# Streaming Conformer layer on one core: the fourth product of odd feed-forward gates placed ahead of the third, and output rows stored from ScalarE's queue

## The chip, the cores and the metric

The kernel runs on one core of a Trainium2 chip. The metric is device time in microseconds (us). The core's engines work in parallel, each through its own instructions in order: TensorE (PE; its weight loads are listed apart as PEld), VectorE (DVE), ScalarE (ACT), GpSimd (POOL) and SyncE (SP), which here does little but issue DMAs. They wait for each other on semaphores. Matrix products end in banks of PSUM; weights and activations lie in SBUF.

## The reference

One layer works on 2048 prompt tokens and 64 sample tokens, all in fp32:

```
h = rms_norm(x) * (1 + sc1) + sh1                  # sc, sh, gt come from c @ w_ada
glu_a, glu_b, q, k, v, g_conv, g_attn = split(h @ w_in)
conv_out = silu(layer_norm(dwconv31(glu_a * sigmoid(glu_b)))) @ w_conv_out
attn_out = band_attention(norm(q), norm(k), v) @ w_attn_out    # 64-token chunks, own and 8 before
merged = sigmoid(g_conv) * conv_out + sigmoid(g_attn) * attn_out
x  = x + gt1 * (merged @ w_o)
h2 = rms_norm(x) * (1 + sc2) + sh2
gate, up = split(h2 @ w_ffn_in)                    # 2 x 2816 columns
y  = x + gt2 * ((silu(gate) * up) @ w_ffn_out)
```

`D_MODEL` is 1024. The outputs are y for both token sets, and the new convolution, key and value states.

## The kernel before

**Products.** Every fp32 weight is split into a high part (`whi`, made by ScalarE) and the rest (`wlo`, made by GpSimd, or by VectorE where the planner finds GpSimd too far behind). A product of fp32 matrices is then three matmuls: high by high, low by high, high by low.

**Stages.** The first part, up to about 1300 us, does the modulation, the input projection, convolution and attention for all tokens. Then three blocks of columns (tokens 0 to 576, 576 to 1344, 1344 to 2112, called blocks 0, 1 and 2) go one after the other through the merge (weights `ca`, matmuls `ps<-cin`), the output projection (`w_o`, matmuls `pw<-whi,m`), the residual and norm, and the feed-forward. The last half tiles of a block's feed-forward, the stores of its output and the loads of the next block's merge weights meet at the border of two blocks.

**The feed-forward.** Its 2816 columns are 22 gates f of 128. Gate and up projection of one f are done together with seven products instead of eight: sums of weight halves (`s1` to `s4`) and plain halves (`a11`, `a12`, `a22`) are multiplied with sums and plain halves of the activations (`t1` to `t4`, `b11`, `b21`, `b22`), each for half of the block's columns (288 in block 0, 384 in the others), twelve matmuls a product. `up` (line 1926) issues them. From f = 5 on (`EARLY`), s2, s1 and s4 of a gate add to one bank, `y`, which the a11 product of the gate before has begun; s3 and a22 add to a second one, `z`; a12 has a third, `x`. ScalarE copies `y` to `u2` after s2 and `z` to `v` after s3; s1 adds to `y` and so waits for the copy `u2`. VectorE adds `y` to `v` after s1, makes c1 from `x` after a12, and multiplies gate and up. The hidden rows are then multiplied with `w_ffn_out`: in block 0 by `down` after each pair of gates (matmuls `pd<-whi,hid`, added to `acc` by VectorE), in blocks 1 and 2 by `down_pair`, whose pieces lie between the products of the next pair at the places of `dn_at`; `down` ends each block.

**Order.** `up_operands` gives the order of the seven products, `weight_order` the order in which weight slabs are staged (two operands of `up_operands` to a slab, low and high, five slabs held), and `up` must follow it. Loads go out on SyncE's queue. Every DMA of SyncE and ScalarE takes one of eight hardware semaphores in turn (`DMAHW0` to `DMAHW7`), and waits for the DMA eight places before it. The planner (`stream`) places prefetches and stores in program order by its own estimate of time; the stores of the output rows (line 2021) are placed by `stream.at` some time after VectorE's last addition.

Of the kernel before, what the change touches and what calls it, by code (L numbers as in the profile page):

```python
# [28 lines left out]
NF = FFN // P  # L29
# [30 lines left out]
EARLY = 5  # L60
PAIRS = range(4, NF - 2, 2)
# [17 lines left out]
def tile_chunks(lo, hi):  # L79

    tiles = token_tiles(lo, hi)
    t, n = tiles[(len(tiles) + 1) // 2 - 1]
    return [(lo, t + n), (t + n, hi)]
# [24 lines left out]
class Lane:  # L108
# [17 lines left out]
    def step(self, entry):  # L126
        try:
            got = next(entry[0])
        except StopIteration:
            self.gens.remove(entry)  # L130
            return
        entry[1], entry[2] = got if isinstance(got, tuple) else (got, {})
# [407 lines left out]
def up_operands(f):  # L540

    ops = (["s2", "s3", "s1"] if f else ["s3", "s2", "s1"]) + ["a12"] * (f >= EARLY) + ["a22"] + ["a11"] * (EARLY <= f + 1 < NF) + ["s4"]
    return [(f + (op == "a11"), op) for op in ops]


def dn_at(f):

    return (0, 1, 3, 6 if f == PAIRS[-1] else 4)  # L550


def mod_order():
# [34 lines left out]
def streaming_layer(ctx: ExitStack, tc: tile.TileContext, I, O):  # L588
    nc = tc.nc
# [8 lines left out]
    y_p, y_s, cs_p, ks_p, vs_p, cs_s, kn_s, vn_s = O  # L598
    y_p, y_s, cs_p, cs_s = y_p[0], y_s[0], cs_p[0, 0], cs_s[0, 0]
# [4 lines left out]
    def rows(prompt, sample, t, n):  # L604
        return prompt[t - SMP : t - SMP + n] if t >= SMP else sample[t : t + n]
# [459 lines left out]
    def half_piece(i, name):  # L1065
        return (wc, wk)[i].tile([P, CW // 2], F32, tag=f"tg{i}", name=name, bufs=2 + i)
# [532 lines left out]
    def piece(tag, name):  # L1599
        return wk.tile([P, CW // 2], F32, tag=tag, name=name, bufs={"t1": 2, "t2": 3}[tag])  # L1600
# [117 lines left out]
    c0, c1 = tile_chunks(*CBLOCKS[0])  # L1718
# [3 lines left out]
    for s, (lo, hi) in enumerate(CBLOCKS):  # L1722
# [60 lines left out]
        def product(ps, w, b, first, last):  # L1783

            for k in range(4):
                mm3(
                    ps[:, :half], w[0][:, k], w[1][:, k], hs[b][0][:, k, :half], hs[b][1][:, k, :half],
                    first and k == 0, last and k == 3, skip_group_check=True,
                )

        def bank(tag):
            return ps_g.tile([P, 512], F32, tag=tag, name="ps", bufs=4)[:, :half]

        def copy(dst, src):
            stream.after("act", "pe")
            act.activation(dst, src, AF.Copy)

        def plus(dst, ps, b):
            stream.after("dve", "pe", "act")
            dve.tensor_tensor(dst, ps, b, ALU.add)  # L1800

        def silu(dst, z):

            tg = half_piece(0, "tg")[:, :half]
            stream.after("act", "pe", "dve")
            act.activation(tg, z, AF.Tanh, scale=0.5)
            stream.after("dve", "act")
            dve.scalar_tensor_tensor(dst, tg, 1.0, z, ALU.add, ALU.mult)
# [25 lines left out]
        def plain(f, i, ps):  # L1834
            hidden(f, i, ps)
            yield 1
# [83 lines left out]
        def rest_of_late(n=99):  # L1920
            while late and n:
                n -= 1
                if next(late[0], None) is None:
                    late.pop(0)

        def up(f, ops, at):
            def step(ps, op, b, first, last, e=f):
                product(ps, ops.use(e, op), b, first, last)
                ops.done()

            if f < EARLY:
                s1, c1 = (t[:, :half] for t in early[f])
                y = bank("y")
            else:
                y, s1 = begun.pop(f)
                c1 = s1

            z = None
            if not f:
                z = bank("y")  # L1940
                step(z, "s3", "t3", True, False)
            step(y, "s2", "t2", f < EARLY, False)
            rest_of_late(1)
            u2 = piece("t1", "u2")[:, :half]
            keep = (lambda dst, ps: plus(dst, ps, s1)) if f < EARLY else copy
            keep(u2, y)
            if f % 2:
                at(3)
            if f:
                z = bank("y")  # L1950
                step(z, "s3", "t3", True, False)
            v = half_piece(1, "v")[:, :half]
            keep(v, z)
            rest_of_late()
            if f % 2 == 0:
                at(0)
            step(y, "s1", "t1", False, False)
            plus(v, y, v)
            if f % 2:
                at(4)  # L1960
            if f >= EARLY:
                x = bank("gp")
                step(x, "a12", "b21", True, True)
                plus(x, x, s1)
                silu(c1, x)
            if f % 2 == 0:
                at(1)
            step(z, "a22", "t4", False, True)
            plus(z, z, u2)
            two = s and f - f % 2 in PAIRS  # L1970
            dve.tensor_tensor(z, z, c1, ALU.mult)
            if EARLY <= f + 1 < NF:
                ny = bank("y")
                step(ny, "a11", "b11", True, False, f + 1)
                begun[f + 1] = ny, piece("t2", "s1")[:, :half]
                copy(begun[f + 1][1], ny)
            for _ in paired(f, 0, z, c1) if two else [hidden(f, 0, z)]:
                pass
            step(y, "s4", "b22", False, True)
            if f < EARLY:  # L1980
                plus(y, y, s1)
            silu(y, y)
            dve.tensor_tensor(y, y, v, ALU.mult)
            late.append(paired(f, 1, y, v) if two else plain(f, 1, y))

        def down(fs, ws):

            last = fs[-1] == NF - 1
            for i, (t, n) in enumerate(tiles):
                if fs[0] == 0:  # L1990
                    acc[i] = token_row("acc")
                pss = [ps_g.tile([P, 512], F32, tag="gp", name="pd", bufs=4) for _ in range(2)]
                gt = gt2[int(t < SMP)] if last else None
                final = last and hi == T and i == len(tiles) - 1
                x1 = [x1s[q // 3][:n, q % 3] for q in (2 * i, 2 * i + 1)] if last else None
                if final:
                    for j in range(2):
                        dst = acc[i][:n, 512 * j : 512 * j + 512]
                        dve.tensor_tensor(dst, dst, gt[:n, 512 * j : 512 * j + 512], ALU.mult)
                        dve.tensor_tensor(dst, dst, x1[j], ALU.add)  # L2000
                for e, j in [(e, j) for e in fs for j in range(2)] if last and not i else [(e, j) for j in range(2) for e in fs]:
                    h = rows_of(e, t, n)
                    f = slice(512 * j, 512 * j + 512)
                    w = ws[e - fs[0]]
                    mm3(pss[j][:n], *h, w[0][:, 0, f], w[1][:, 0, f], e == fs[0], e == fs[-1])
                for j, ps in enumerate(pss):
                    f = slice(512 * j, 512 * j + 512)
                    dst = acc[i][:n, f]
                    stream.after("dve", "pe")
                    if fs[0] == 0:  # L2010
                        act.activation(dst, ps[:n], AF.Copy)
                    elif not last:
                        dve.tensor_tensor(dst, dst, ps[:n], ALU.add)
                    else:
                        if not final:
                            dve.tensor_tensor(ps[:n], ps[:n], dst, ALU.add)
                        dve.tensor_tensor(ps[:n], ps[:n], gt[:n, f], ALU.mult)
                        dve.tensor_tensor(dst, ps[:n], dst if final else x1[j], ALU.add)
                        stream.at(
                            stream.when("dve") + OUT_LAG,  # L2020
                            lambda t=t, n=n, f=f, dst=dst: nc.sync.dma_start(rows(y_p, y_s, t, n)[:, f], dst),
                        )
            for _ in fs:
                W.done()
# [30 lines left out]
        for f in range(0, NF, 2):  # L2055
            ops = Operands(f)
# [5 lines left out]
            def at(i, f=f):  # L2062
                if s and f - 2 in PAIRS:
                    if i in dn_at(f - 2):
                        down_pair(f - 2, dn_at(f - 2).index(i))
                elif i == 0 and 2 <= f <= NF - 4:
                    down([f - 2, f - 1], [W.get(("fo", e)) for e in (f - 2, f - 1)])
# [48 lines left out]
```

## Time and profile before

| | us |
|---|---|
| median of 3 runs | 3044.03 (3043.26 to 3046.47) |
| the profiled execution's own time | 3045.71 |
| its span | 3043.9 |
| TensorE busy | 2932.8 |
| VectorE busy | 1996.2 |
| ScalarE busy | 1321.8 |
| GpSimd busy | 984.2 |

Busy time overlaps between engines. A row of the timeline gives the start in us, the duration, engine, line, operation, output<-inputs by the program's names, shapes and a count where rows of one kind are folded; in brackets stand the idle time of the engine before it and what ended it. Nearly all rows have line L103, that of the helper which records each instruction, so the names tell them apart: `ps<-t` is a product with t1 to t4, `ps<-b` one with b11, b21 or b22, `pd<-whi,hid` is the down-projection, `u<-ps` and `v<-ps` are ScalarE's copies, `out<-acc` are the output stores, `tg<-g_d` loads of the merge's gates. A q behind an engine's name (SPq) means its queue of issued DMAs.

### The profile page before, as it was taken

Reading aid. Unit: us, or ns where it says so; the run is one execution under the profiler, and the core shown is the slowest. Engines: PE = TensorE matmul, PEld = TensorE weight load, DVE = VectorE, ACT = ScalarE, POOL = GpSimd, SP = SyncE. Lnnn points to the kernel's source line nnn. Section 1 sums busy time; section 2 is a strip of 40 time slices with the busy share of each in tenths; the row PEclk is TensorE's granted clock in tenths of the full one; section 3 lists DMA queues with packets and bytes.
Section 4 is the critical chain, followed back from the end, with each engine's and each line's share of the span. In section 5 each row is a group of like instructions: output and inputs, shape, how many; then the busy total and the mean of one; then the engine's idle time right before and its main releaser. Section 6 shows DMA issues by size and latency. Waiting matters only on the chain. (4 is left out here: it accounts for less than half of the span.)

```text
span 3043.9 us, 44749 instructions
## 1 busy us (share of the span) xinstructions
PE 2932.8 (96%) x16259; PEld 2609.7 (86%) x16259; DVE 1996.2 (66%) x3595; ACT 1321.8 (43%) x2371; POOL 984.2 (32%) x617
## 2 busy tenths in 40 slices
PE   7989898999999999989999999999999999999998
PEld 4889776887888888878989889999999898999997
DVE  5896687667956895566666755655666756366567
ACT  3334542563365257463444425534444244333332
POOL 1200120101011102345677433247767341333331
PEclk9999998999999999999999999999999999999999
DMA  9788798877997788886444786455556965355544
GB/s 304 261 278 285 254 298 296 273 246 264 299 289 222 267 270 267 257 278 216 148 144 143 233 283 206 159 164 190 184 194 202 340 213 191 118 167 174 166 161 176
DMA packets 487018, 690.97 MB, mean 227 GB/s; under 512 B 38420, under 2 KB 316808, under 8 KB 486797
## 3 DMA queue, kind: packets, MB, share of 16 engines
q1 hardware_dynamic: 474517, 670.72, 67.2%
q10 hardware_dynamic: 12280, 17.39, 1.6%
q8 instruction: 128, 2.10, 0.3%
q14 instruction: 93, 0.76, 0.1%
HBM read 503.79 MB, written 184.19 MB: 226 GB/s over the span
## 5 line engine op out<-in xcount | busy, mean ns | idle before, releaser
L103 POOL TENSOR_TENSOR wlo<-wst,whi 128x1024 fp32r<-128x1024 f32 (+1 forms) x180 | 401.7, 2238 | 497.6 <-ACT whi L103 452.2
L103 PE MATMUL ps<-t,whi 128*128 128x384 f32 (+1 forms) x2112 | 507.4, 325 | 10.9 <-DVE t L103 5.2
L103 PE MATMUL pd<-whi,hid 128*128 128x512 f32 (+1 forms) x1400 | 450.6, 392 | 3.3 <-DVE acc L103 3.3
L103 ACT ACTIVATE whi<-wst 128x1024 fp32r<-128x1024 f32 (+1 forms) x273 | 266.1, 979 | 356.7 <-PE ps L103 123.4
L103 PE MATMUL ps<-b,whi 128*128 128x384 f32 (+1 forms) x1584 | 381.1, 326 | 11.6 <-DVE pw L103 4.0
L103 PEld LDWEIGHTS ps<-t,whi 128*128 128x128 f32 x2112 | 371.8, 190 | 19.2 <-DVE t L103 6.2
L103 DVE SCALAR_TENSOR_TENSOR y<-u,wd,y 128x512 f32<-128x512 f32 (+1 forms) x480 | 369.2, 773 | 8.2
L103 PE MATMUL ps<-hh,whi 128*128 128x512 f32 (+2 forms) x992 | 364.5, 367 | 1.0 <-DMA whi<-w_din_h 0.8
L103 PE MATMUL ps<-hl,whi 128*128 128x512 f32 (+2 forms) x992 | 346.9, 350 | 0.0
L103 PE MATMUL ps<-hh,wlo 128*128 128x512 f32 (+2 forms) x992 | 346.9, 350 | 0.0
L103 DVE TENSOR_TENSOR acc<-acc,pd 128x512 f32<-128x512 f32 (+1 forms) x440 | 290.7, 684 | 80.5 <-PE pd L103 76.7
L103 PE MATMUL ps<-t,wlo 128*128 128x384 f32 (+1 forms) x1056 | 341.6, 324 | 0.0
L103 PEld LDWEIGHTS pd<-whi,hid 128*128 128x128 f32 (+1 forms) x1400 | 258.4, 185 | 64.4 <-DVE acc L103 6.8
L103 PEld LDWEIGHTS ps<-b,whi 128*128 128x128 f32 x1584 | 277.9, 189 | 14.9 <-DVE pw L103 4.3
L103 PE MATMUL pd<-wlo,hid 128*128 128x512 f32 (+1 forms) x700 | 274.1, 392 | 0.0
L103 PE MATMUL ps<-b,wlo 128*128 128x384 f32 (+1 forms) x792 | 257.4, 325 | 0.0
L103 ACT ACTIVATE pr<-pr,sm 128x640 f32<-128x640 f32 (+3 forms) x272 | 200.1, 747 | 128.1 <-DVE sm L103 126.2
L103 POOL TENSOR_TENSOR r<-t,mhalf 128x1 f32<-128x1 f32 (+3 forms) x68 | 82.2, 1211 | 412.8 <-DVE t L103 369.1
L103 PEld LDWEIGHTS ps<-hh,wlo 128*128 128x128 f32 x992 | 188.2, 190 | 22.5 <-issue 0.4
L103 POOL TENSOR_TENSOR wlo<-wup,whi 128x1024 fp32r<-128x1024 f32 (+1 forms) x64 | 138.2, 2161 | 212.5 <-ACT whi L103 196.7
L103 PEld LDWEIGHTS ps<-hh,whi 128*128 128x128 f32 x992 | 189.1, 191 | 20.0 <-issue 2.7
L103 PEld LDWEIGHTS ps<-hl,whi 128*128 128x128 f32 x992 | 189.1, 191 | 15.5 <-issue 1.7
(215 smaller groups left out, 5719.6 us busy)
## 6 DMA issues: line engine op xcount, KB each, us to landing
whi<-w_din_h SPq DMA_DIRECT2D x72, 512.0 KB, 4.1
wlo<-w_din_l SPq DMA_DIRECT2D x72, 512.0 KB, 7.1
wst<-sum_d SPq DMA_DIRECT2D x131, 256.0 KB, 2.9
wmod<-in_w_ada SPq DMA_DIRECT2D x48, 512.0 KB, 7.2
sum_d<-ws SPq DMA_DIRECT2D x88, 256.0 KB, 2.5
wst<-in_w_ffn_in SPq DMA_DIRECT2D x85, 256.0 KB, 3.5
wst<-in_w_in SPq DMA_DIRECT2D x40, 512.0 KB, 7.4
wst<-in_w_ffn_in SPq DMA_DIRECT2D x37, 512.0 KB, 5.5
```

Source lines behind the costliest of these rows:

```text
L103: return f(*args, **kw)
```

## The change

In odd gates from f = 5 on, the product a12 with what VectorE and ScalarE make of it moves ahead of s1, and the operands' order with it, so that the slabs of such a gate are (s3, a12) and (s1, a22) instead of (s3, s1) and (a12, a22). The last piece of `down_pair`, B22, stays behind s1, at the fifth slab's place instead of the fourth's. Even gates keep their order. The 34 output stores are issued by ScalarE instead of SyncE.

```diff
@@ up_operands, dn_at
-    ops = (["s2", "s3", "s1"] if f else ["s3", "s2", "s1"]) + ["a12"] * (f >= EARLY) + ["a22"] + ["a11"] * (EARLY <= f + 1 < NF) + ["s4"]
+    ops = (["s2", "s3"] if f else ["s3", "s2"]) + ["a12"] * (f >= EARLY and f % 2) + ["s1"] + ["a12"] * (f >= EARLY and f % 2 == 0) + ["a22"] + ["a11"] * (EARLY <= f + 1 < NF) + ["s4"]
     return [(f + (op == "a11"), op) for op in ops]
...
-    return (0, 1, 3, 6 if f == PAIRS[-1] else 4)
+    return (0, 1, 3, 6 if f == PAIRS[-1] else 5)
@@ up
+            def factor():
+                if f >= EARLY:
+                    x = bank("gp")
+                    step(x, "a12", "b21", True, True)
+                    plus(x, x, s1)
+                    silu(c1, x)
+
             if f % 2 == 0:
                 at(0)
+            else:
+                factor()
             step(y, "s1", "t1", False, False)
             plus(v, y, v)
             if f % 2:
-                at(4)
-            if f >= EARLY:
-                x = bank("gp")
-                step(x, "a12", "b21", True, True)
-                plus(x, x, s1)
-                silu(c1, x)
-            if f % 2 == 0:
+                at(5)
+            else:
+                factor()
                 at(1)
             step(z, "a22", "t4", False, True)
@@ down
-                            lambda t=t, n=n, f=f, dst=dst: nc.sync.dma_start(rows(y_p, y_s, t, n)[:, f], dst),
+                            lambda t=t, n=n, f=f, dst=dst: nc.scalar.dma_start(rows(y_p, y_s, t, n)[:, f], dst),
```

First place: TensorE in an odd gate of block 0. Of each product the first matmul is shown, or the first that waits; t3, t1, b21 and t4 belong to s3, s1, a12 and a22, b11 to a11 of the next gate. First before, then the change.

```order
L103 MATMUL ps_16850<-t3_13835,wlo_16727 128x288 [waits Pool_49]
...
L103 MATMUL ps_16784<-t1_13829,whi_16726 128x288 [waits Activation_49]
...
L103 MATMUL ps_16883<-b21_12991,wlo_16733 128x288 [waits Pool_49]
...
L103 MATMUL ps_16850<-t4_13837,whi_16732 128x288 [waits Activation_49]
...
L103 MATMUL ps_16920<-b11_12989,whi_16770 128x288 [waits DVE_49]
```

```order
L103 MATMUL ps_16850<-t3_13835,wlo_16727 128x288 [waits Pool_49]
...
L103 MATMUL ps_16869<-b21_12991,wlo_16727 128x288
...
L103 MATMUL ps_16784<-t1_13829,whi_16732 128x288 [waits Activation_49]
...
L103 MATMUL ps_16850<-t4_13837,whi_16732 128x288 [waits Activation_49]
...
L103 MATMUL ps_16920<-b11_12989,whi_16770 128x288 [waits DVE_49]
```

The twelve matmuls of a12 have moved ahead of the twelve of s1; all else stands as before. The split of the weights changes with it: 27 low parts, two per pair of gates in block 0 and two in block 1, are made by VectorE and not by GpSimd.

Second place: the queues at the border of blocks 0 and 1. Before, on SyncE, the last weights of block 0's and the first of block 1's, two of the ten stores, and what follows them:

```order
L381 DMA wst_18124<-in_w_attn_out 128x4x128 [waits DMAHW5_49]
L2021 DMA out_1<-acc_14383 64x512 [waits DMAHW6_49,DVE_49]
...
L2021 DMA out_0<-acc_14475 128x512 [waits DMAHW7_49,DVE_49]
L1071 DMA tg_18272<-g_d_68 128x384 [waits DMAHW0_49,DVE_49]
...
L381 DMA wst_18309<-in_w_attn_out 128x4x128 [waits DMAHW7_49]
L381 DMA wst_18312<-in_w_o 128x1024 [waits DMAHW0_49,DVE_49]
L1071 DMA tg_18323<-g_d_68 128x384 [waits DMAHW1_49]
```

With the change, on ScalarE, the last of the hidden rows, then the stores between the splits of the next merge weights:

```order
L103 ACTIVATE hid_13825<-ps_17835 128x288 [waits DVE_49]
L2026 DMA out_1<-acc_14383 64x512 [waits DMAHW5_49,DVE_49]
...
L2026 DMA out_0<-acc_14456 128x512 [waits DMAHW3_49,DVE_49]
L103 ACTIVATE whi_18234<-wup_17946 128x1024 [waits DMAHW7_49,PE_49,Pool_49]
L2026 DMA out_0<-acc_14475 128x512 [waits DMAHW7_49,DVE_49]
L103 ACTIVATE whi_18238<-wst_18084 128x1024 [waits DMAHW4_49,DMAHW5_49,PE_49,Activation_49]
L2026 DMA out_0<-acc_14475 128x512 [waits DMAHW2_49,DVE_49]
L103 ACTIVATE whi_18242<-wst_18120 128x1024 [waits DMAHW3_49,DMAHW1_49,DMAHW6_49,PE_49,Activation_49]
```

Eight stores stand ahead of the split of the second merge weight, one each ahead of the third's and fourth's. On SyncE the loads of `tg` and of the merge weights now follow each other directly, and two loads of `tg` that came behind the first weight of `w_o` come ahead of it.

Third place: TensorE in the same border's merge. Before, the first matmul of the output projection stands between the fifth and sixth merge weights' products:

```order
L103 MATMUL ps_18433<-cin_18015,wlo_18247 128x384
L103 MATMUL pw_18584<-whi_18423,m_18225 128x512 [waits Activation_49]
L103 MATMUL ps_18456<-cin_18014,whi_18289 128x384 [waits DVE_49]
...
L103 MATMUL pw_18584<-wlo_18424,m_18225 128x512 [waits Pool_49]
L103 MATMUL ps_18475<-cin_18015,whi_18289 128x384 [waits DVE_49]
```

With the change it stands behind the last of them:

```order
L103 MATMUL ps_18555<-cin_18015,whi_18377 128x384
L103 MATMUL ps_18555<-cin_18017,whi_18377 128x384
L103 MATMUL ps_18555<-cin_18015,wlo_18378 128x384
L103 MATMUL pw_18584<-whi_18421,m_18225 128x512 [waits Activation_49]
L103 MATMUL pw_18584<-wlo_18422,m_18225 128x512 [waits Pool_49]
```

Two matmuls have moved, from among the merge's products to behind them.

## The prediction

> **What bounds the kernel now.** I began with the page: busy shares, then the chain that ended last, by engine.
>
> ```profile
> PE 2932.8 (96%) x16259; PEld 2609.7 (86%) x16259; DVE 1996.2 (66%) x3595; ACT 1321.8 (43%) x2371; POOL 984.2 (32%) x617
> PE 40%; DVE 2%; DMA 1%; issue 1%; ACT 0%; SPq 0%; POOL 0%; DVEq 0%; ACTq 0%; POOLq 0%
> ```
>
> TensorE is busy for 96% and leads the chain. The change removes no matmul, so it can only win back idle time of TensorE: 3043.9 - 2932.8 = 111 us over the whole span. Then I took the view by stretches for the three feed-forward loops (columns: length, then busy us and count of PE, PEld, DVE, ACT and POOL, the granted clock, DMA share, GB/s).
>
> ```profile
> 1450.00:1706.00 256.00, 252.14 (x1594) 229.33 (x1594) 165.14 (x246) 103.58 (x211) 176.35 (x119) 1.00 0.45 143
> 2010.00:2370.00 360.00, 360.00 (x1905) 339.47 (x1904) 217.10 (x374) 166.02 (x280) 245.93 (x143) 1.00 0.59 193
> 2645.00:3000.00 355.00, 355.00 (x1882) 335.23 (x1881) 211.88 (x367) 133.59 (x222) 139.41 (x59) 1.00 0.50 163
> ```
>
> In blocks 1 and 2 TensorE has no gap at all; a new order of products has nothing to win there. Block 0 leaves 3.9 us in seven pairs of gates. One pair's stretch, the waits of that loop, and the timeline around one odd gate say where:
>
> ```profile
> 1522.66:1559.26 36.60, 36.05 (x228) 32.84 (x229) 23.52 (x36) 14.88 (x31) 25.64 (x18) 1.00 0.46 145
> PEld ps L103 <- ACT u L103: 5.5, 7, 0.8
> PE ps L103 <- ACT u L103: 3.9, 7, 0.6
> 1520.37 0.42 PE L103 MATMUL ps<-t,whi 128*128 128x288 f32 x2
> 1522.66 0.53 PE L103 MATMUL ps<-t,whi 128*128 128x288 f32 x2 [0.55 <-ACT u L103]
> 1524.35 0.42 PE L103 MATMUL ps<-b,whi 128*128 128x288 f32 x2
> 1525.93 0.43 PE L103 MATMUL ps<-t,whi 128*128 128x288 f32 x2
> 1521.90 0.41 ACT L103 ACTIVATE hid<-ps 128x288 fp32r<-128x288 f32 x1 [2.18 <-DVE ps L103]
> 1522.20 0.41 ACT L103 ACTIVATE u<-ps 128x288 f32<-128x288 f32 x1
> 1523.44 0.41 ACT L103 ACTIVATE v<-ps 128x288 f32<-128x288 f32 x1
> ```
>
> The four PE rows start, in turn, s3, s1, a12 and a22 of an odd gate. An unhindered product takes 1525.93 - 1524.35 = 1.58 us. From s3 to a12 two products take 3.98 us, not 3.16: s1 may not add to the shared bank before ScalarE has copied it to u (1522.20 + 0.41 = 1522.61), and TensorE starts 0.05 us later. The gap shows as 0.55, but the odd gate loses 0.82.
>
> The other loss in reach is between blocks 0 and 1, from the chain of waits in order of time, with the same stage one block later (the two rows from 2401.79) as a yardstick:
>
> ```profile
> 1761.71 0.52 PE L103 MATMUL ps<-cin,whi 128*128 128x384 f32 x2
> 1761.88 2.13 PE ps L103 x12
> 1802.18 27.47 PE pw L103 x121
> 2401.79 8.76 PE ps L103 x48
> 2436.81 27.90 PE pw L103 x123
> 1784.65 0.50 PE L103 MATMUL pw<-whi,m 128*128 128x512 f32 x1 [1.58 <-ACT whi L103]
> 1789.55 0.50 PE L103 MATMUL pw<-wlo,m 128*128 128x512 f32 x1 [2.29 <-POOL wlo L103]
> 1790.00:1795.00 5.00, 5.00 (x22) 5.00 (x21) 2.14 (x5) 1.44 (x2) 0.40 (x1) 0.66 0.85 311
> ```
>
> Twelve matmuls of the merge take 2.13 us, 0.1775 each; its 192 are worth 34.1 us. At the first boundary they take 1802.18 - 1761.71 = 40.5 (the first row is their first), at the second 2436.81 - 2401.79 = 35.0. So 6.4 us are lost at the first and 0.9 at the second. Of the 6.4, 1.58 and 2.29 are gaps before two matmuls of the output projection (pw) that stand among the merge's products; the rest is their start-up and the clock, granted at 0.66 right after.
>
> **The change part by part.** *Odd gates.* a12 now stands between s3 and s1. s1 would start at 1520.37 + 2 x 1.58 = 1523.53, and u is ready at 1522.61: 0.92 us of slack. What could be late next? a22 starts at 1525.11 and needs ScalarE's v copy, done at 1523.85: 1.26 us of slack. So the loop should gain 7 x 0.82 = 5.8 us, bounds 0 and 5.8.
>
> Against this, the new order moves two splits per pair (wlo, 128x512) from GpSimd to VectorE, in block 0 and in block 1:
>
> ```profile
> L103 DVE TENSOR_TENSOR wlo<-ws,whi 128x512 fp32r<-128x512 f32 x34 | 42.6, 1253 | 4.9 <-ACT whi L103 2.6
> 1534.62 1.51 DVE L103 TENSOR_TENSOR wlo<-ws,whi 128x512 fp32r<-128x512 f32 x2 [0.27 <-ACT whi L103]
> 1536.05 1.42 DVE L103 TENSOR_TENSOR acc<-acc,pd 64x512 f32<-64x512 f32 x2
> 1533.83 0.39 PE L103 MATMUL pd<-whi,hid 128*64 128x512 f32 x1
> 1536.83 0.39 PE L103 MATMUL pd<-wlo,hid 128*128 128x512 f32 x1
> ```
>
> They cost 0.75 to 1.25 us each, 1.5 to 2.5 a pair. VectorE is busy for 165 of 256 us in that loop, so the time is there; the one tight place is the down-projection. From its first matmul to the one at 1536.83 there are thirteen, 0.231 us each; a tile has twelve, so the third tile starts near 1533.83 + 24 x 0.231 = 1539.37. It needs the banks that VectorE frees at 1536.05 + 1.42 = 1537.47: 1.9 us of slack against up to 2.5, so up to 0.6 a pair, 4.2 us in seven, if the whole 2.5 falls just there. I take 0, as the splits stand ahead of the down-projection on VectorE, beside TensorE's products. In block 1 the products hide the two splits as well; uncovered they would be 2.5 a pair, 20 us in eight pairs, but with VectorE idle for 143 of 360 us there I bound them at one pair's worth, 2.5 us, and take 0.
>
> *The stores.* These rows show SyncE's queue, ScalarE and VectorE at the first boundary.
>
> ```profile
> 1762.71 8.97 SPq L2021 DMA_DIRECT2D out<-acc  x10
> 1771.77 1.08 SPq L1071 DMA_DIRECT2D tg<-g_d  x2
> 1777.77 1.02 SPq L381 DMA_DIRECT2D wst<-in_w_o  x1
> 1778.84 0.90 SPq L1071 DMA_DIRECT2D tg<-g_d  x2
> 1783.98 0.56 DVE L103 SCALAR_TENSOR_TENSOR t<-tg,ps 128x384 f32<-128x384 f32 x1 [4.59 <-DMA tg<-g_d]
> 1737.76 0.41 ACT L103 ACTIVATE hid<-ps 128x288 fp32r<-128x288 f32 x1 [1.87 <-DVE ps L103]
> 1759.87 1.06 ACT L103 ACTIVATE whi<-wup 128x1024 fp32r<-128x1024 f32 x1 [21.70 <-PE pd L103]
> 1761.40 1.06 ACT L103 ACTIVATE whi<-wst 128x1024 fp32r<-128x1024 f32 x1 [0.47 <-DMA wst<-in_w_attn_out]
> 1761.01 2.42 POOL L103 TENSOR_TENSOR wlo<-wup,whi 128x1024 fp32r<-128x1024 f32 x1 [27.55 <-ACT whi L103]
> 1757.94 0.69 DVE L103 TENSOR_TENSOR acc<-pd,x 128x512 f32<-128x512 f32 x1
> 1725.00:1745.00 20.00, 20.00 (x119) 16.76 (x118) 14.96 (x25) 7.20 (x12) 2.40 (x1) 1.00 1.03 334
> 1785.00:1790.00 5.00, 2.71 (x15) 2.35 (x14) 3.68 (x6) 1.56 (x2) 4.50 (x2) 1.00 1.02 386
> ```
>
> Ten stores hold SyncE's queue for 8.97 us; the gate tiles (tg) and weights behind them start that much later, and VectorE waits 4.59 us for a tg. Taken off this queue, those loads can be issued up to 9 us earlier. On ScalarE eight stores fall into its 21.70 us of idle time before 1759.87, as the eighth's rows are done at 1757.94 + 0.69 = 1758.63. The ninth and tenth stand ahead of the splits of the third and fourth merge weights. Second effect: the two pw matmuls no longer stand among the merge's products but behind them, so their weights are wanted near 1761.71 + 34.1 = 1795.8 and not at 1784.65, and both gaps go.
>
> What need not go is the wait for tg before the sixth merge product (t is done at 1784.54; the matmuls ahead end at 1783.07): the DMA engines are full there (share 1.02), so stores from another queue still take bytes. But one 512 KB load of w_o no longer stands ahead of that tg, worth 0.524 MB / 386 GB/s = 1.4 us, which alone brings t to 1783.2. So I give back 4.9 of the 6.4 us and leave 1.5 for what remains of it; bounds -6.4 and +5 (the slow rival). At the second boundary, 0.9 lost to one tg wait, I take -0.3, bounds -0.9 and +2. The end of the kernel is set by VectorE's last tiles; the last store leaves from an idle queue either way: 0.
>
> **Sum.** -5.8 - 4.9 - 0.3 = -11.0 us on the profiled 3045.71: 3034.7. The shown median is 1.68 below the profiled run, so 3033.0.
>
> **The rivals.** (1) *Only the loop gains.* The full DMA engines speak for it: same bytes, same landing times, so tg comes only the 1.4 us sooner, the merge stalls elsewhere instead, and the sum is -5.8 - 1.4 = -7.2, or 3036.8; with a little of the loop lost to the two splits, 3038.5, at the edge of what can be told. The Trainium skill, "DMA: Bandwidth & Descriptors", section "Issuing engines are not separate DMA queues", says that DMAs of different issuing engines share the same 16 DMA engines, so that another issuer saves only issue time. By that rule this rival's price is the right one for the boundary; the share of 1.02 agrees that the engines are full. Against it: the gaps of 1.58 and 2.29 us come from the place of two matmuls, which moves.
>
> (2) *Nothing measurable.* The splits put back 4.2 + 2.5 us and the boundary stays as it is: -5.8 + 6.7 = +0.9, 3045. For it: the 1.9 us of slack; against: VectorE idles a third of the loop.
>
> (3) *Slower: ScalarE stands behind a store.* A store that waits for a free DMA slot holds all of ScalarE. If the eighth is held past 1759.87, the split of the second merge weight, GpSimd's 2.42 us behind it and the merge slip. TensorE wants that weight at 1761.71 + 4.26 = 1765.97, and GpSimd is done at 1763.43: it decides beyond 2.5 us of delay. The same ten stores took 8.97 us on SyncE; as long a hold costs 8.97 - 2.5 = 6.5 on top of today's loss at the first boundary, and as much at the second: -5.8 + 13.0 = +7.2, 3051. Against it: the eight have 21.70 us of idle ScalarE, and the down-projection yields their rows one by one, not in a burst.
>
> **How the numbers follow.** Chances: forecast 0.62 (3033.0, its own range 3029 to 3037.5), only the loop 0.22 (3036.8 to 3040, half of it under 3038), nothing 0.08, slower 0.08. A change of 0.2% is 6.1 us, about what a measurement of this kernel can tell from none; faster means below 3037.9. So faster 0.62 + 0.11 = 0.73, within 0.2% 0.11 + 0.08 = 0.19, slower 0.08. The range 3029 to 3041 leaves out the last two cases and a sliver below, 0.18.
>
> **What would show it.** In block 0, pairs of 35.8 instead of 36.60 us, and no wait of TensorE on u. If the wait returns as one on acc before the third down tile, the splits were mis-sized. At the first boundary: the pw matmuls behind the merge, its stage about 35.6 us long, SyncE's queue without the 9 us of stores, no clock below 1.00. If the stage still takes 40 us with waits on tg, rival 1 holds; if ScalarE's splits start late behind a store, rival 3. Blocks 1 and 2 should keep full stretches; a gap there would make the forecast wrong in sign.

## The result

Over 19 runs of each, the changed kernel takes 3036.07 us (median) and the one before 3042.82. The ratio is 0.9981, 95% interval 0.9972 to 0.9989, or 5.8 us less (3.3 to 8.5); the two medians differ by 6.8. The forecast was 11.0 us. The time lies in the range given; the gain is about half of what the sum said, and sits at the 0.2% that a measurement can just tell.

Single runs of one and the same kernel spread over 11 us (before) and 14 us (after) here. The traces show where most of it comes from: the first down-projection matmul of block 0, ahead of which TensorE's order is unchanged, starts anywhere between 1387 and 1400 us in the thirteen profiles of this study. Two profiles of the change itself differ by 7.4 us, 5.1 of them ahead of that point. So the stages behind that point are compared trace by trace.

From the profile after the change, first the stretches of the three loops (columns as before), then the starts of s3, a12 and s1 of an odd gate on TensorE:

```profile
1450.00:1706.00 256.00, 256.00 (x1638) 234.74 (x1637) 179.15 (x264) 104.91 (x218) 162.88 (x110) 1.00 0.46 146
2010.00:2370.00 360.00, 360.00 (x1902) 339.23 (x1901) 224.28 (x388) 163.00 (x277) 222.03 (x126) 1.00 0.60 200
2645.00:3000.00 355.00, 355.00 (x1875) 334.43 (x1874) 214.28 (x371) 133.21 (x221) 134.73 (x58) 1.00 0.51 164
...
1519.11 0.42 PE L103 MATMUL ps<-t,whi 128*128 128x288 f32 x2
1520.69 0.43 PE L103 MATMUL ps<-b,whi 128*128 128x288 f32 x2
1522.27 0.42 PE L103 MATMUL ps<-t,whi 128*128 128x288 f32 x2
```

The loop of block 0 is as full as the others now, and products follow each other every 1.58 us. Next the two merges: the first matmul of each, the first gaps, and the pieces of the chain in which the output projection begins.

```profile
1755.77 0.52 PE L103 MATMUL ps<-cin,whi 128*128 128x384 f32 x2
1765.57 0.44 PE L103 MATMUL ps<-cin,wlo 128*128 128x384 f32 x1 [0.81 <-POOL wlo L103]
1776.31 0.62 PE L103 MATMUL ps<-cin,whi 128*128 128x384 f32 x2 [0.24 <-DVE m L103]
1779.50 0.59 PE L103 MATMUL ps<-cin,whi 128*128 128x384 f32 x2 [0.80 <-DVE t L103]
1792.61 27.90 PE pw L103 x123
2393.14 0.62 PE L103 MATMUL ps<-cin,whi 128*128 128x384 f32 x2 [0.57 <-DVE acc L103]
2408.48 0.62 PE L103 MATMUL ps<-cin,whi 128*128 128x384 f32 x2 [2.36 <-DVE m L103]
2431.47 27.92 PE pw L103 x123
```

The first merge takes 1792.61 - 1755.77 = 36.8 us (40.5 before), the second 2431.47 - 2393.14 = 38.3 (35.0 before). In the first the two gaps at pw matmuls are gone and three small ones have come, and the stretch at a granted clock of 0.66 did not return: every 5 us from 1750 to 1805 show 1.00. In the second there is a new gap of 2.36 us, on the merged columns m. The ledger of these two profiles, from the first down-projection of block 0 to the last matmul (the loop of block 0 is counted to the start of the closing down-projection, 1395.51 to 1734.41 before; block 1 from the end of the second half of its merge to the next merge):

| stage | before, us | after, us | difference |
|---|---|---|---|
| block 0, first to closing down-projection | 338.9 | 333.4 | -5.5 |
| first merge (192 matmuls) | 40.5 | 36.8 | -3.6 |
| block 1 | 531.4 | 531.9 | +0.5 |
| second merge | 35.0 | 38.3 | +3.3 |
| all that lies between and behind these | 694.9 | 695.5 | +0.6 |
| sum | 1640.7 | 1636.0 | -4.7 |

### The profile page after: what moved, and what is told of

It reads as the page before. It is cut to its first block, busy times and chain, and to the rows that moved or that the text cites. A ratio compares the mean times of both kernels' runs of the same rounds, so it can differ in the third digit from the quotient of the medians.

```text
span 3039.1 us, 44723 instructions
## 1 busy us (share of the span) xinstructions
PE 2930.2 (96%) x16259; PEld 2605.9 (86%) x16259; DVE 2014.6 (66%) x3622; ACT 1320.2 (43%) x2371; POOL 948.9 (31%) x590
## 4 chain that ended last, share of the span: by engine, by line
PE 76%; DVE 10%; DMA 7%; issue 2%; ACT 2%; POOL 1%; SPq 1%; ACTq 0%; DVEq 0%; POOLq 0%
PE ps L103 49%; PE pd L103 14%; PE pw L103 6%; DVE y L103 4%; PE sc L103 2%; PE po L103 2%; PE ptp L103 2%; DVE wlo L103 1%; DMA kk<-k_d 1%; DMA cin<-o_d 1%; DMA x<-x_d 1%; PE pt L103 1%; DVE pr L103 1%; PE pa L103 1%; POOL r L103 1%
## 5 line engine op out<-in xcount | busy, mean ns | idle before, releaser
L103 POOL TENSOR_TENSOR wlo<-wst,whi 128x1024 fp32r<-128x1024 f32 (+1 forms) x170 | 386.4, 2277 | 524.5 <-ACT whi L103 484.0
```

What stands on the lines that cost most here:

```text
L103: return f(*args, **kw)
```

## The experiments

Two theories were set against each other after the result. **A** is the forecast: the stores held up the loads behind them on SyncE's queue, so taking them off that queue helps both merges. **B**: the first merge gains by the new place of the two pw matmuls; the stores, issued as early as their rows are ready, go ahead of the merge's weights and gates on DMA engines that are already full, and cost time at both borders.

This table has the stages of all kernels (TensorE rows, read as above) and, where it was timed, the ratio to before.

| kernel | block 0 loop | first merge | second merge | ratio (95%) |
|---|---|---|---|---|
| before | 338.9 | 40.5 | 35.0 | |
| the change | 333.4 | 36.8 | 38.3 | 0.9981 (0.9972 to 0.9989) |
| the change again (e14) | 333.4 | 35.1 | 38.0 | 0.9981 (0.9971 to 0.9991) |
| e1, new order only | 333.4 | 38.2 | 35.0 | 0.9976 (0.9965 to 0.9987) |
| e2, stores on ScalarE only | 339.1 | 35.8 | 38.3 | 0.9991 (0.9982 to 1.0000) |
| e7, block 1's stores on SyncE | 333.7 | 34.7 | 34.2 | 0.9975 (0.9964 to 0.9986) |
| e4, no stores in blocks 0 and 1 | 333.9 | 34.1 | 34.2 | |
| e9, an eighth of the bytes | 333.7 | 34.1 | 34.2 | |
| e8, stores on GpSimd | 333.8 | 36.0 | 40.3 | 1.0001 (0.9988 to 1.0013) |
| e5, late stores on SyncE | 333.8 | 34.1 | 34.2 | 0.9962 (0.9951 to 0.9974) |
| e5 again (e12) | 333.4 | 34.1 | 34.2 | 0.9976 (0.9964 to 0.9988) |
| e10, old order, late stores | 339.1 | 34.1 | 34.2 | 0.9982 (0.9971 to 0.9993) |
| e13, as e5, splits back to GpSimd | 340.7 | 34.1 | 34.2 | 0.9998 (0.9988 to 1.0009) |

**The parts alone.** The new order with the stores on SyncE:

```diff
-   lambda t=t, n=n, f=f, dst=dst: nc.scalar.dma_start(rows(y_p, y_s, t, n)[:, f], dst),
+   lambda t=t, n=n, f=f, dst=dst: nc.sync.dma_start(rows(y_p, y_s, t, n)[:, f], dst),
```

> Only the order of odd gates; the output stores stay on SyncE's queue. Both theories: no wait of TensorE on u in block 0, its loop 5.5 us shorter. The order of TensorE shows the two pw matmuls behind the merge's products here too. Theory A (on record: the stores must leave SyncE's queue): at the first boundary tg still comes late behind 9 us of stores, the merge's stage stays near 39 to 40 us, the whole gains about 6. Theory B (the gain at the first boundary comes from the place of the two pw matmuls, and the stores on ScalarE cost at the second): first stage about 37 us, second 35 as before, the whole gains 8 to 10 and is faster than the full change by 2 to 4 us.

And the kernel before with that line the other way round, `nc.sync` to `nc.scalar`:

> Only the stores on ScalarE; the old order of products. Both: seven waits on u remain, 5.5 us. Theory A: the first merge stage about 36.8 us, the second no longer than 35.5, the whole gains 4 to 5. Theory B: first about 37, second about 38 as ScalarE's copies m wait behind splits whose weights land late, the whole gains 0 to 1 us.

e1's only gap in the first merge, and the waits of TensorE in e2's loop of block 0 with its gap in the second merge:

```profile
1775.92 0.98 PE L103 MATMUL ps<-cin,whi 128*128 128x384 f32 x2 [2.38 <-DVE t L103]
```

```profile
PE ps L103 <- ACT u L103: 3.9, 7, 0.6
...
2404.92 0.62 PE L103 MATMUL ps<-cin,whi 128*128 128x384 f32 x2 [2.36 <-DVE m L103]
```

The loop gains by the order alone: seven waits on u in e2, none in e1. The first merge gains from either part (38.2 and 35.8 from 40.5), and in both kernels the two pw matmuls stand behind the merge, so part of this gain may come with their place. The whole loss in the second merge is the stores': 38.3 in e2 with the old order, to a tenth that of the full change. e1 alone is not slower than the whole change, but the 2 to 4 us by which theory B had it faster are not there either (0.9976 against 0.9981). Theory A had both merges gain by the stores' move and falls for the second. Theory B stands, though its 37 us for e1's first merge was 1.2 short: with the stores on SyncE a tg still comes late there, which is A's mechanism and real, and behind that gap the granted clock was 0.80 (1777.1 to 1782.1).

**Block 1's stores put back.**

```diff
-   nc.scalar.dma_start(rows(y_p, y_s, t, n)[:, f], dst)
+   (nc.sync if s == 1 else nc.scalar).dma_start(rows(y_p, y_s, t, n)[:, f], dst)
```

> The full change, with block 1's twelve stores back on SyncE. Theory A: second merge stage between 35 and 38 us. Theory B: second stage 35.0 us and no wait of TensorE on m, first stage as with the full change (36.8): 3 us faster than the full change.

```profile
2392.61 34.19 PE ps L103 x192
2426.80 27.92 PE pw L103 x123
```

The chain of waits shows the second merge in one piece of 192 matmuls with no gap: 34.2 us. The time, 3033.80, is 2.3 us below the change's, where 3 were expected; the intervals overlap, and the trace carries the verdict.

**Which property of the stores it is.** ScalarE's store rows can hurt in three ways: ScalarE stands in order behind a store that waits for one of the eight DMA slots; the slots themselves are taken; the bytes go ahead of the weights. No stores at all in blocks 0 and 1 give the floor:

```diff
-   stream.at(
+   hi == T and stream.at(
```

> The full change with the 22 output stores of blocks 0 and 1 left out, so that these output rows are not written: the floor of the two borders. If the stores are the cause of what remains of the stalls, both merge stages take 34.0 to 34.5 us; if full DMA engines from other transfers are, the first stays above 35.5 and the second above 36.

Stores of 64 columns in place of 512 keep instructions, places and slots, and take most of the bytes away:

```diff
-   nc.scalar.dma_start(rows(y_p, y_s, t, n)[:, f], dst)
+   nc.scalar.dma_start(rows(y_p, y_s, t, n)[:, f][:, : 512 if hi == T else 64], dst[:, : 512 if hi == T else 64])
```

> The full change, but each store of blocks 0 and 1 writes 64 of its 512 columns, so that the rest of these rows is not written: the same instructions, places and waits on ScalarE, an eighth of the bytes. If it is the bytes ahead of the merge weights that delay them, both stages fall to 34 to 35 us as without stores. If it is the eight DMA slots taken in turn and ScalarE standing in order behind a store, the second stage stays at 37 to 38 us.

Stores from GpSimd keep the bytes and their early time, but take eight semaphores of their own, not the eight that SyncE and ScalarE share, and leave ScalarE free:

```diff
-   nc.scalar.dma_start(rows(y_p, y_s, t, n)[:, f], dst)
+   nc.gpsimd.dma_start(rows(y_p, y_s, t, n)[:, f], dst)
```

> The full change with the 34 stores on GpSimd's queue: full bytes at the same early time, but not behind ScalarE's splits. If the bytes alone delay the merge weights: second stage 37 to 38 us, time as with the full change. If ScalarE's order and the eight slots do: 34 to 35 us and 3 us faster than the full change.

The second merge of e9 in its chain, and there the split that was late after the change:

```profile
2385.08 34.19 PE ps L103 x192
...
2388.78 1.06 ACT L103 ACTIVATE whi<-wup 128x1024 fp32r<-128x1024 f32 x1 [3.85 <-DMA out<-acc]
```

The same split and its followers after the change, with SyncE's issue of a merge weight:

```profile
2400.31 0.51 SPq L381 DMA_DIRECT2D wst<-in_w_attn_out  x1
2403.77 1.06 ACT L103 ACTIVATE whi<-wup 128x1024 fp32r<-128x1024 f32 x1 [10.78 <-DMA wup<-in_w_attn_out]
2406.40 1.06 ACT L103 ACTIVATE whi<-wst 128x1024 fp32r<-128x1024 f32 x1 [1.57 <-DMA wst<-in_w_attn_out]
2407.36 0.47 ACT L103 ACTIVATE m<-ps 128x384 fp32r<-128x384 f32 x1
```

And e8's wait in the second merge, with its load of the same weight (us to landing at the end):

```profile
PE ps L103 <- DVE m L103: 3.5, 1, 3.5
...
2392.48 1.88 SPq L381 DMA_DIRECT2D wup<-in_w_attn_out  x1
...
wup<-in_w_attn_out SPq DMA_DIRECT2D x1, 256.0 KB, 11.3
```

The name in e9's bracket misleads. The split waits for its weight, whose load SyncE issued at 2382.54 and whose semaphore is full at 2388.67; the two stores next to it were issued at 2385.06 and 2385.66, as soon as VectorE had their rows. So no store holds ScalarE there. In all six kernels below this split starts when its weight has landed, and what differs is when that is. In us from the first matmul of the second merge:

| kernel | SyncE issues the load | the split starts |
|---|---|---|
| before | -5.8 | 3.9 |
| the change | 3.0 | 10.6 |
| e9, an eighth of the bytes | -2.5 | 3.7 |
| e8, stores on GpSimd | 1.5 | 12.9 |
| e7, block 1's stores on SyncE | -6.6 | 3.1 |
| e5, late stores | -6.5 | 3.2 |

After the change, ScalarE's copy m, which frees a bank for TensorE, stands behind that split and the next one and comes at 2407.36, 14.2 us into the merge: TensorE waits 2.36 us. In e8 neither ScalarE nor the eight slots are touched by stores, and the second merge is the longest of all, 40.3. GpSimd, which issues the stores there, is not what is late: it stands idle for 8.91 us until ScalarE has made that split. So it is the bytes, put ahead of the weights, that delay the merge, and issuing them from GpSimd in place of ScalarE does not help. Thin stores also land sooner and so free their slots sooner, which e9 alone could not tell apart; e8 does. As an estimate: ten stores leave ahead of the weight's load, 2.62 MB, and at the 361 GB/s of that stretch they are worth 7.3 us; the split is 6.7 us later than before (10.6 against 3.9). Why e8 is 2 us worse than the change is not shown.

How the bytes delay the weight in the change itself stands in SyncE's waits from 2371 to 2411 us:

```profile
SPq L381 <- DMA cin<-c_d: 5.2, 2, 2.8
SPq L1079 <- DMA out<-acc: 5.1, 2, 2.8
SPq L381 <- DMA cin<-o_d: 3.3, 1, 3.3
```

SyncE stands still until the stores and the loads of `cin` have landed that hold the slots which its next loads need; before, none of these waits is there. In e8 it waits for no store, and the loads are late all the same.

The gap is not all of the loss: 38.3 is 4.1 above the 34.2 us of e4. Two stretches of 5 us behind the gap (columns as before):

```profile
2408.00:2413.00 5.00, 4.52 (x17) 4.52 (x18) 4.92 (x8) 2.49 (x3) 1.97 (x2) 0.66 1.06 383
2415.00:2420.00 5.00, 5.00 (x30) 5.00 (x29) 2.96 (x7) 2.05 (x4) 2.74 (x2) 1.00 0.93 325
```

At a granted clock of 0.66, 17 matmuls ran where 4.52 us at full rate hold 27; the ten are worth 1.8 us at 0.1775 each, an estimate, and 2.36 + 1.8 makes up the 4.1.

The issues of DMAs at the second border say the same. First before (2370 to 2415 us), then after the change (2370 to 2410): count, KB each, median us from issue to landing.

```profile
out<-acc SPq DMA_DIRECT2D x12, 256.0 KB, 4.0
```

```profile
out<-acc ACTq DMA_DIRECT2D x12, 256.0 KB, 7.1
```

All twelve are issued in either window, but a store takes 7.1 us to land when it runs beside the loads of `cin` and the weights, and 4.0 behind them.

**The stores late.** If the stores should go behind the loads, place them there. On SyncE's queue, placed by the planner 40 us behind VectorE's last addition instead of 4:

```diff
-OUT_LAG = 4000.0
+OUT_LAG = 40000.0
...
-   lambda t=t, n=n, f=f, dst=dst: nc.scalar.dma_start(rows(y_p, y_s, t, n)[:, f], dst),
+   lambda t=t, n=n, f=f, dst=dst: nc.sync.dma_start(rows(y_p, y_s, t, n)[:, f], dst),
+   hi != T,
```

(The last argument keeps the planner from issuing them when it closes the block.)

> The new order of products; the 22 stores of blocks 0 and 1 on SyncE's queue, but some 40 us later, behind the merge weights and the tg loads. If the stores take the DMA engines from the merge's loads (theory B), both merge stages fall to 34.1 to 35 us and the whole gains 10 to 13 us against before. If the loads are late for a reason other than the stores (full DMA engines from the prefetches), the stages stay near 36 to 37 and 35.

The same lateness with the old order of products:

> The old order of products; the 22 stores of blocks 0 and 1 late on SyncE's queue. If place and time of the stores set both borders alone: stages of 34 to 35 us both, the seven waits on u remain, 6 to 7 us faster than before. If the first border also needs the new order of products, its stage stays above 37.

The two merges of e5 in the chain of waits:

```profile
1755.04 33.92 PE ps L103 x192
...
2389.64 34.19 PE ps L103 x192
```

Both merges run without a gap, as if there were no stores, and e10 shows that this needs nothing of the new order. The first border's 6.4 us were all to be had: about two thirds by the stores' bytes and queue place (38.2 in e1 to 34.1 in e5), one third with the new order, in which the pw matmuls change their place (40.5 to 38.2). That the place alone is worth this third is not shown, as no run moves it alone.

Run once more beside the full change:

> The same kernel as e5_late_sp, once more beside the full change on one chip. If late stores on SyncE are what the full change lacked, both merge stages take 34 us again and it is 5 to 7 us faster than the full change (2.7 us of the first stage, 4.1 of the second).

> The full change itself, on the same chip: first merge stage 35.5 to 37 us, second 38, 6 to 8 us faster than before.

The stages repeat: 34.1 and 34.2 against 35.1 and 38.0. The medians are 3034.44 and 3036.26, and the ratios to before (table) overlap: by time alone, late stores cannot be told from the change. By trace they save 4.1 us on the stretch from block 0's first down-projection to the last matmul (1629.5 against 1633.6), less than the 5 to 7 expected. The first merge of the change itself moved between 36.8 and 35.1 from one profile to the other, and is 34.7 in e7, which leaves that border as it is; so the 3.6 us above carry about 2 us of uncertainty.

**The splits.** Many of VectorE's splits back to GpSimd, on top of e5:

```diff
-BEHIND = 4000.0
+BEHIND = 8000.0
```

> As e5_late_sp, but VectorE takes a split over only where GpSimd is twice as far behind, so that most splits go back to GpSimd. If the splits on VectorE are free, as predicted, the loop of block 0 stays at 333.4 to 333.9 us and blocks 1 and 2 stay as they are. If they cost something in block 1, it gets 0.5 to 1 us shorter.

TensorE's waits in its loop of block 0:

```profile
PE ps L103 <- ACT s L103: 2.1, 1, 2.1
PE pd L103 <- DVE acc L103: 2.1, 1, 2.1
PE ps L103 <- DVE v L103: 1.3, 2, 0.8
PE ps L103 <- ACT u L103: 0.8, 1, 0.8
```

This went the other way: the loop takes 340.7 us, 7.3 more than e12's, and by time nothing of what e5 gained is left. But it is a larger step than the change's own: in this loop VectorE makes 39 low parts, against 89 in e12 and 77 before. So it shows that moving fifty of them back costs time here, and does not price the twelve that the change moved in this loop. The gaps are of two kinds. At the end of the loop GpSimd's splits stand in the chain of waits ahead of the ones of 0.83 (on u) and 2.09 us (on s). The wait on acc is the one that the prediction feared, two splits on VectorE ahead of the addition that frees the bank:

```profile
1600.37 6.27 DVE L103 TENSOR_TENSOR wlo<-ws,whi 128x512 fp32r<-128x512 f32 x2 [0.97 <-ACT whi L103]
...
1607.29 0.50 PE L103 MATMUL pd<-whi,hid 128*128 128x512 f32 x1 [2.05 <-DVE acc L103]
```

There the two took 6.27 us, where the prediction had up to 2.5; why they were so slow was not followed further.

## Why the prediction was half right

**The loop, -5.8: right.** It measured -5.5 (338.9 to 333.4; 7 x 0.82 is 5.74, not 5.8). s1 starts where the prediction put it, 3.16 us behind s3, and from 1430 us on TensorE has no wait on u, v or acc. The price of 0 for the two moved splits held in block 0. In block 1, first to last down-projection takes 444.3 us in the three kernels of the old order and 444.7 in the nine of the new one with the splits on VectorE, so 0.5 of the 2.5 us bound. Most of it is not the splits: e13, which has none of them on VectorE there, still takes 444.6, and block 2, where none moved, went from 444.3 to 444.6 as well. A new order of products had nothing to win in full stretches, as the prediction said, and it cost about 0.3 us in each, a term that the sum did not have.

**The first border, -4.9: size right within the spread, mechanism half right.** It measured -3.6 in one profile of the change, -5.4 in the other and -5.8 in e7. The pw matmuls did move, their gaps went, and the low clock behind them. What failed is "Taken off this queue, those loads can be issued up to 9 us earlier". VectorE multiplies each tg into a tile `t`. The load of tg for the fourth `t` was issued 17.1 us after the merge's first matmul before, and 17.4 and 15.5 us after it in the two profiles of the change; with late stores (e5) it was 10.3. The stores had left SyncE's queue, but not the slots that it shares with ScalarE: around this border SyncE's loads of weights waited 5.2 us for stores to land, and 9.5 in the second profile. The fourth `t` before, after the change, and in its second profile (e14):

```profile
1783.98 0.56 DVE L103 SCALAR_TENSOR_TENSOR t<-tg,ps 128x384 f32<-128x384 f32 x1 [4.59 <-DMA tg<-g_d]
```

```profile
1778.82 0.54 DVE L103 SCALAR_TENSOR_TENSOR t<-tg,ps 128x384 f32<-128x384 f32 x1
```

```profile
1772.00 0.54 DVE L103 SCALAR_TENSOR_TENSOR t<-tg,ps 128x384 f32<-128x384 f32 x1
```

Counted from the first matmul of the merge that is 22.3 us before, and 23.1 and 21.3 after. So "worth 1.4 us" for the load of w_o that no longer stands ahead of that tg is neither shown nor refuted: the two profiles lie 0.8 later and 1.0 sooner. With late stores (e5) it is 16.7. The whole 6.4 us were there for a change that moved the bytes.

**The second border, -0.3 with bounds -0.9 and +2: wrong, +3.3.** This is the term that took the other half of the gain. The step that failed is the term: it was taken from the one tg wait of 0.9 us there, as if the stores could hardly do harm, and no row stood behind the +2. Before, the twelve stores stood behind six loads of the merge's weights on SyncE's queue (2394.04 to 2403.71, the stores from 2404.54 on), and that order protected them: SyncE's queue had been doing the sorting by urgency. On ScalarE the first eight are issued as soon as VectorE has finished their rows and a slot is free, from 14.4 us before the merge on, and nobody waits for them:

```profile
2378.77 12.24 ACTq L2026 DMA_DIRECT2D out<-acc  x8
```

**The sum.** By the two profiles -4.7 was measured in place of -11.0. Of the 6.3 us that are missing the second border took 3.6, the first 1.3, the loop 0.3, and 1.1 lies outside these terms. That the time fell into the range is a gain at one border and a loss at the other, partly luck; so is that it came out beside rival 1's 3036.8, whose parts (-5.8, -1.4 and nothing) were not the measured ones.

**The rivals.** Rival 1 (the bytes are the same, only the issuer changes) named the right mechanism. It was too mild: it let the first border gain 1.4 us and the second lose nothing, while early bytes take time from those that are waited for. The Trainium skill, "DMA: Bandwidth & Descriptors", section "Issuing engines are not separate DMA queues", was the rule to follow there. The runs agree with it: from ScalarE and from GpSimd the early stores lengthen the second merge alike, to 38.3 and 40.3 us. Rival 3 (ScalarE behind a store) did not come. At the first border a row looks like it:

```profile
1753.96 0.38 SPq L381 DMA_DIRECT2D wst<-in_w_attn_out  x1
1762.00 1.06 ACT L103 ACTIVATE whi<-wst 128x1024 fp32r<-128x1024 f32 x1 [6.96 <-DMA out<-acc]
```

```profile
1746.50 0.38 SPq L381 DMA_DIRECT2D wst<-in_w_attn_out  x1
1754.57 1.06 ACT L103 ACTIVATE whi<-wst 128x1024 fp32r<-128x1024 f32 x1 [4.54 <-DMA wst<-in_w_attn_out]
```

The second pair is the same split in the second profile of the change. In both it starts 8.0 to 8.1 us after the load of its weight was issued; in the first that load's semaphore is full at 1761.90, and the store ahead of the split had been issued at 1756.67. So the wait of 6.96 us is for the weight, not for a store, and TensorE's 0.81 us behind it are the price of a load issued late. The eighth store had left by 1753.06, ahead of the split at 1753.98. Rival 2 did not come: the loop kept its gain.

## What to carry to other kernels

Where the DMA engines are full, as at the second border here, moving a transfer that nobody waits for to an idle issuing engine does not hide it; it lets it pass the transfers that are waited for. Ask of each store what is queued behind it on the DMA engines, and what waits for its slot, not only what stands on its issuer's queue, and give it a late place instead. When a bracket names a DMA, look up which load the waiting instruction reads before building on the name. And where a gain is summed over two similar places, look up what protects each of them today: the second border had little to win and an order worth keeping.

## What the runs showed of the hardware that was not expected

The landing time of a 256 KB store went from 4.0 to 7.1 us by issuing the same twelve among other loads; the DMA engines were full in both (105.2% of 16 engines before, 84.0% and 20.7% by two queues after). A gap of 2.36 us on TensorE was followed by a granted clock of 0.66 and cost about 4.1 us in all, while gaps of 0.8 us and less at the first border left it at 1.00. A store to GpSimd's queue was no cheaper for the merge than one to ScalarE's (40.3 against 38.3 us). And the first 1390 us of the program, the same instructions in the same order on TensorE, ended up to 13 us apart in the thirteen profiles of this study (1387 to 1400 us); what makes them differ was not studied.
